# Gate and up from seven products of halves instead of eight, and one weight ring for the feed-forward

## The chip, the cores and the metric

The kernel runs on one core of one Trainium2 chip. The metric is the device time of one execution in microseconds, lower is better. Below, PE is the matrix engine TensorE, DVE is VectorE, ACT is ScalarE, POOL is GpSimd and SP is the engine whose queue starts the DMAs, in order.

## What is computed

One layer of a hybrid encoder over 2048 tokens of width 1024, in float32:

```
a    = rms_norm(h, ln_mix_pre)
proj = a @ w_in                      # split by columns into four mixers
mix  = concat([s5, hgrn2, fox, mlstm]) @ w_out
h    = h + rms_norm(mix, ln_mix_post)
a    = rms_norm(h, ln_ffn_pre)
ff   = (silu(a @ w_ffn_gate) * (a @ w_ffn_up)) @ w_ffn_down
h    = h + rms_norm(ff, ln_ffn_post)
```

w_ffn_gate and w_ffn_up are 1024 x 2816, w_ffn_down is 2816 x 1024, w_out 1024 x 1024. The change concerns the last four lines.

## The kernel before

**Stages.** The in-projection (`in_proj`, to about 840 us) runs over two halves of the tokens and, in each, over chunks of the columns of w_in; between chunks, hooks of a dictionary place other work (the S5 set-up, the mixers of the first tokens, and `first`, which does `Attn.pre(0)` and `Attn.proj(0)`). Then the feed-forward section runs over four blocks of 512 tokens: for block b the projection `attn.proj(b)`, the mixers of block b + 1, and the feed-forward `run(b)`, with `attn.pre(b + 1)` near its end. A scheduler of the language orders the instructions of each engine by its own timeline; the mixers of the next block are so spread between the products of this one. The last block has no mixers beside it.

**Precision.** Every float32 operand is kept as two parts, hi and lo, in the matmul type F32R, and a product takes three matmuls per 128 rows of depth: hi x hi, hi x lo, lo x hi. A weight tile is split at its first use (`split_load`): a copy by ACT gives hi (L89), a subtraction by POOL lo (L90); both parts are stored to DRAM, and later blocks load them (L85). Activations are split too (L104, L105) and both parts are transposed by PE, 4 tiles of 128 x 128 at a time (`transpose_parts`, L109), and copied out of PSUM by ACT and DVE (L112, L114).

**Attention projection** (`Attn.proj`, L1394): the first 512 columns of w_out for all four token tiles, then the second 512, one token tile after the other. After each tile follow its norm, the residual (its x loaded by L1427 into `b_xt`, a ring of two buffers), the store of h1 (L1429), the second norm (L1340, L1423, L1428, L69, L70, L1433) and the transposes.

**Feed-forward.** `gate_up` (L1477) makes for each of the 22 f tiles of 128 columns gate and up of all 512 tokens: 8 k x 3 parts x 2 = 48 matmuls of 512 columns. The first two f tiles of a block are done together in two halves of 256 columns, tokens 0 to 255 first (`cuts`). `down` (L1502) multiplies two f tiles at a time with w_ffn_down, 48 matmuls of 512 columns, and DVE adds the result to the accumulator (L1507). Gate and up weights go through a ring of 4 pairs of 128 x 1056, those of w_ffn_down through one of 4 pairs of 128 x 512.

## Time and profile before

| | us |
|---|---|
| median of 3 runs | 2833.97 |
| lowest and highest | 2827.44, 2839.25 |
| profiled execution, its time | 2835.35 |
| profiled execution, its span | 2833.6 |
| PE busy in the span | 2720.2 (96%) |
| DVE, POOL, ACT busy | 1598.5, 883.9, 830.7 |
| DMA moved | 605.11 MB, mean 214 GB/s |

The profile is one execution, taken by the hardware profiler. Busy times of the engines overlap. PEld is the loading of weights into PE, which runs beside its matmuls. Since the kernel has stages with different limits, tables by stage say more than the sums; a "window" is a stretch of the span in microseconds.

### The profile page before, as it was taken

The numbers are of one execution on the slowest core, as the hardware profiler recorded it, in microseconds if no ns is written. First come the engines' busy times: TensorE is split into PE (matmuls) and PEld (weight loads), VectorE is DVE, ScalarE is ACT, GpSimd is POOL, SyncE is SP. The second block draws the span as 40 slices with busy tenths as digits, with TensorE's granted clock in tenths as the row PEclk, the third lists the DMA queues.
The fourth block names the chain that finished last, engine by engine and source line by source line (L and its number), as shares of the span: only waits on it lengthen the run. The fifth ranks groups of instructions, "written<-read, shape, count | busy, mean of one in ns | idle before, by whom it ended". The sixth has DMA issues, their size and how long they took to land.

```text
span 2833.6 us, 40116 instructions
## 1 busy us (share of the span) xinstructions
PE 2720.2 (96%) x14678; PEld 2294.8 (81%) x14678; DVE 1598.5 (56%) x2587; ACT 830.7 (29%) x1596; POOL 883.9 (31%) x959
## 2 busy tenths in 40 slices
...
GB/s 201 207 255 135 179 289 171 169 176 154 254 191 313 279 270 252 242 295 230 288 164 210 192 207 212 153 264 210 214 184 188 196 170 230 273 211 193 190 192 139
DMA packets 323108, 605.11 MB, mean 214 GB/s; under 512 B 56160, under 2 KB 146144, under 8 KB 322656
## 3 DMA queue, kind: packets, MB, share of 16 engines
...
q0 software_dynamic: 1024, 0.07, 0.0%
...
## 4 chain that ended last, share of the span: by engine, by line
PE 72%; DVE 11%; DMA 9%; issue 3%; POOL 2%; SPq 2%; ACT 2%; DVEq 0%; POOLq 0%; ACTq 0%
PE pf L1477 30%; PE pf L1502 15%; PE pf L297 6%; PE pf L279 5%; PE pf L1394 3%; PE ps L912 2%; DMA g_h<-h_d 1%; DVE hQ L520 1%; DMA b_xt<-in_x_dram 1%; PE ps L896 1%; PE ps L895 1%; PE ps L837 1%; DVE hA L534 1%; PE pt L109 1%; DVE xl L105 1%
## 5 line engine op out<-in xcount | busy, mean ns | idle before, releaser
L1477 PE MATMUL pf<-b_ah,wl 128*128 128x512 f32 (+1 forms) x1536 | 580.0, 378 | 0.0
L1477 PE MATMUL pf<-b_ah,wh 128*128 128x512 f32 (+1 forms) x1536 | 579.6, 378 | 0.3 <-DMA wh<-wg2h 0.3
L1477 PE MATMUL pf<-b_al,wh 128*128 128x512 f32 (+1 forms) x1536 | 579.7, 379 | 0.0
L1502 PE MATMUL pf<-dh,g_h 128*128 128x512 f32 x1408 | 458.8, 395 | 1.9 <-DVE b_acc L1507 1.8
L1477 PEld LDWEIGHTS pf<-b_ah,wh 128*128 128x128 f32 x1536 | 290.4, 189 | 55.0 <-issue 0.4
L1477 PEld LDWEIGHTS pf<-b_ah,wl 128*128 128x128 f32 x1536 | 290.5, 189 | 54.8
L1477 PEld LDWEIGHTS pf<-b_al,wh 128*128 128x128 f32 x1536 | 289.6, 189 | 54.3
L1502 PEld LDWEIGHTS pf<-dh,g_h 128*128 128x128 f32 x1408 | 263.3, 188 | 57.5 <-DVE b_acc L1507 2.9
L1502 PE MATMUL pf<-dl,g_h 128*128 128x512 f32 x704 | 276.5, 393 | 0.0
L1507 DVE TENSOR_TENSOR b_acc<-b_acc,pf 128x512 f32<-128x512 f32 x320 | 215.6, 683 | 102.1 <-PE pf L1502 100.2
L909 POOL TENSOR_TENSOR f_accs<-f_accs,f_pe 128x512 f32<-128x512 f32 (+3 forms) x144 | 172.4, 1197 | 285.0 <-ACT f_pe L903 281.8
L90 POOL TENSOR_TENSOR wl<-wr,wh 128x1024 fp32r<-128x1024 f32 (+2 forms) x76 | 187.5, 2471 | 223.6 <-ACT wh L89 194.9
L905 DVE TENSOR_TENSOR f_pl<-f_pe,f_ph 128x512 fp32r<-128x512 f32 (+3 forms) x160 | 187.0, 1176 | 94.5 <-ACT f_ph L904 78.2
L297 PE MATMUL pf<-wh,aTh 128*128 128x256 f32 (+2 forms) x768 | 219.8, 287 | 2.6 <-ACT stg L323 1.6
L297 PE MATMUL pf<-wl,aTh 128*128 128x256 f32 (+2 forms) x768 | 221.4, 288 | 0.0
L297 PE MATMUL pf<-wh,aTl 128*128 128x256 f32 (+2 forms) x768 | 220.3, 287 | 0.0
L1482 DVE SCALAR_TENSOR_TENSOR g_th<-g_th,pf 128x512 f32<-128x512 f32 x88 | 60.3, 685 | 198.7 <-ACT g_th L1481 198.1
L1481 ACT ACTIVATE g_th<-pf 128x512 f32<-128x512 f32 x88 | 52.7, 599 | 399.1 <-PE pf L1477 399.0
L279 PE MATMUL pf<-aTh,wh 128*128 128x512 f32 (+1 forms) x400 | 159.8, 400 | 1.0 <-ACT hnz L304 1.0
L279 PE MATMUL pf<-aTl,wh 128*128 128x512 f32 (+1 forms) x400 | 158.3, 398 | 2.5 <-DVE aTl L114 2.5
L903 ACT ACTIVATE f_pe<-ps 128x512 f32<-128x512 f32 (+3 forms) x160 | 85.4, 534 | 252.7 <-PE ps L896 106.7
L279 PE MATMUL pf<-aTh,wl 128*128 128x512 f32 (+1 forms) x400 | 159.1, 398 | 0.0
...
## 6 DMA issues: line engine op xcount, KB each, us to landing
...
```

Of the source, the lines that this page charges most:

```text
L90: nc.gpsimd.tensor_tensor(lo, r, f32(hi), ALU.subtract)
L279: nc.tensor.matmul(l3(pt)[:, cut], lhsT=x[k][:, s], rhs=a[:, cut, k], start=(n == 0), stop=(n == 23))
L297: nc.tensor.matmul(pt[:, :w], lhsT=a[:, t, k], rhs=x[k], start=(n == 0), stop=(n == 23))
L903: nc.scalar.activation(pe[:, cs], pt[:, cs], AF.Exp)
L905: nc.vector.tensor_tensor(pl[:, cs], pe[:, cs], f32(ph[:, cs]), ALU.subtract)
L909: nc.gpsimd.tensor_tensor(accs[:, cs], accs[:, cs], pe[:, cs], ALU.add)
L912: nc.tensor.matmul(o, lhsT=w, rhs=r[:, cs], start=(kt + n == 0), stop=(kt + n == NK))
L1394: nc.tensor.matmul(pt, lhsT=a[:, t, k], rhs=w, start=(first and i == 0), stop=(last and i == 2))
L1477: nc.tensor.matmul(l3(pt)[:, s], lhsT=x[:, k], rhs=a[:, s, k], start=(k == 0 and i == 0), stop=(k == KD - 1 and i == 2))
L1482: nc.vector.scalar_tensor_tensor(th, th, 1.0, pts[0], ALU.add, ALU.mult)
L1502: nc.tensor.matmul(pt, lhsT=a[:, s], rhs=w[:, 0], start=(m == 0), stop=(m == 3 * len(fs) - 1))
L1507: nc.vector.tensor_tensor(acc[:, t, ns], acc[:, t, ns], pt, ALU.add)
```

## The change

It has seven parts.

1. Gate and up of two f tiles (a pair q) and both halves of the tokens are a 2 x 2 product of blocks: two halves of the depth (512), two f tiles. It is formed by the scheme of Strassen and Winograd from 7 products of sums instead of 8. A product is 4 k x 3 parts for gate and for up (m), with 256 columns; DVE puts them together with seven additions per pair, and ACT makes one copy.
2. The sums of weights are made in the in-projection (`FfnWeights.make`, 22 units, placed by hooks): two loads of 512 KB, four subtractions or additions of 128 x 512 on POOL, seven stores of 256 KB. Those of products 0, 2 and 5 are split at first use, and the parts stored; those of 1, 3, 4 and 6 are loaded and split in every block.
3. The sums of activations (`Attn.operands`) are made after every second token tile, three on DVE, one on POOL; 7 x 4 transposes follow. Both x tiles of the ring of two are held until then. No f tile is done in halves of the tokens any more.
4. Transposes are of plain float32, once; ACT copies hi out of PSUM, DVE subtracts lo.
5. One ring of 12 pairs of 128 x 512 takes all weights of the section, w_out too; the in-projection's ring is closed with it.
6. w_ffn_down and w_out are copied from DRAM to DRAM (30 copies of 512 KB) by the hooks of the in-projection, and read from the copies. `attn.proj(0)` moves out of the hook to the start of the section.
7. To make room, the mixers beside the feed-forward have fewer or smaller buffers (`hK` 3 and `hQ` 2 instead of 4, the fox pool `p` 4 instead of 5, the `f_KB` ring 2, and the like).

In PE's order at the start of the last block, the rows before are: L1394 is the projection, L109 the transposes, L1477 gate and up with 256 columns.

```order
L1394 MATMUL pf<-dl,b_ah 128x512
L109 MATMUL pt<-identr,xh 128x128 x4
L109 MATMUL pt<-identr,xl 128x128 x4
L109 MATMUL pt<-identr,xh 128x128 x4
L109 MATMUL pt<-identr,xl 128x128 x4
L1477 MATMUL pf<-b_ah,wh 128x256
L1477 MATMUL pf<-b_ah,wl 128x256
```

After, at the same place, L1436 is the projection, L111 the transposes and L1530 the products (g_h holds the sums, b_xt the plain tiles):

```order
L1436 MATMUL pf<-dl,b_U 128x512
L111 MATMUL pt<-ident,g_h 128x128 x4
L111 MATMUL pt<-ident,b_xt 128x128 x4
L111 MATMUL pt<-ident,g_h 128x128 x12
L111 MATMUL pt<-ident,b_xt 128x128 x8
L1530 MATMUL pf<-b_U,dh 128x256
L1530 MATMUL pf<-b_U,dl 128x256
```

Where 16 transposes stood behind the projection's last matmul, 28 stand now, and the first product behind them.

SP's order at the same start of the block, before (L1427 loads x, L1429 stores h1, L85 loads parts of weights):

```order
L1429 DMA h_d_228<-b_acc 128x1024 x2
L1427 DMA b_xt<-in_x_dram 128x1024
L85 DMA wh<-wg1h 128x1024
L85 DMA wl<-wg1l 128x1024
L85 DMA wh<-wu1h 128x1024
L85 DMA wl<-wu1l 128x1024
L1429 DMA h_d_228<-b_acc 128x1024
L85 DMA dh<-wd_0h 128x512
L85 DMA dl<-wd_0l 128x512
L85 DMA dh<-wd_0h 128x512
L85 DMA dl<-wd_0l 128x512
L1427 DMA b_xt<-in_x_dram 128x1024
```

After (L1469 loads x, L81 loads parts, L1376 loads a raw sum, L1618 loads h1 for the end):

```order
L81 DMA dh<-w_2_0h 128x512
L81 DMA dl<-w_2_0l 128x512
L81 DMA dh<-w_2_1h 128x512
L81 DMA dl<-w_2_1l 128x512
L1618 DMA g_h1s<-h_d_375 128x1024
L1376 DMA dl<-ws_3_0_66 128x512
L1376 DMA dl<-ws_3_1_67 128x512
L1376 DMA dl<-ws_4_0_68 128x512
L1376 DMA dl<-ws_4_1_69 128x512
L1376 DMA dl<-ws_6_0_72 128x512
L1376 DMA dl<-ws_6_1_73 128x512
L1469 DMA b_xt<-in_x_dram 128x1024 x2
```

The last two loads of x stood apart from each other, the second behind four loads of w_ffn_down; now both stand behind ten loads of weights of the next products.

SP's order in the third chunk of the in-projection, before (L88 loads w_in, L94 stores its parts; the last row is the third chunk's second load):

```order
L88 DMA wr<-in_w_in_dram 128x4x256
L1006 DMA s_cl<-in_s_lambda_re_dram 16x64 x2
L1010 DMA s_ldt<-in_s_log_dt_dram 128x16
L1067 DMA s_br<-in_s_b_re_dram 64x16x16
L94 DMA wi_1l<-wl 128x1024
L1067 DMA s_br<-in_s_b_re_dram 64x16x16
L1067 DMA s_bi<-in_s_b_im_dram 64x16x16 x2
L88 DMA wr<-in_w_in_dram 128x4x256
```

After (L1717 copies w_ffn_down; L100 loads w_in, L90 stores its parts):

```order
L1717 DMA wd_d<-in_w_ffn_down_dram 16x8192 x4
L90 DMA wi_0l<-wl 128x1024
L100 DMA wr<-in_w_in_dram 128x4x256
L1717 DMA wd_d<-in_w_ffn_down_dram 16x8192 x7
L1008 DMA s_cl<-in_s_lambda_re_dram 16x64 x2
```

Copies of w_ffn_down and w_out have come between the loads of w_in, 28 of the 30 of them ahead of the third chunk's second load.

The diff, cut to these parts:

```diff
...
-def split_load(c, pool, raw, tag, width, shape, src, key=None, part=None):
+def split_load(c, pool, tag, width, n, src, key=None, raw=None):
     nc = c.nc
-    n = shape[0] * shape[1]
     hi = pool.tile([P, width], F32R, name=tag + "h", tag=tag + "h")[:, 0:n]
     lo = pool.tile([P, width], F32R, name=tag + "l", tag=tag + "l")[:, 0:n]
     if key in c.parts:
-        a = part or 0
         for t, d in zip((hi, lo), c.parts[key]):
-            nc.sync.dma_start(f32(t), d[:, a:a + n])
-    else:
-        r = raw.tile([P, width], F32, name=tag + "r", tag=tag + "r")[:, 0:n]
-        nc.sync.dma_start(r.rearrange("p (k n) -> p k n", k=shape[0]), src)
-        nc.scalar.activation(hi, r, AF.Copy)
-        nc.gpsimd.tensor_tensor(lo, r, f32(hi), ALU.subtract)
-        if key is not None:
-            c.parts[key] = kept = [c.dram.tile([P, n], F32, name=f"{key}{x}") for x in "hl"]
-            for t, d in zip((hi, lo), kept):
-                nc.sync.dma_start(d, f32(t))
-    return [x.rearrange("p (k n) -> p k n", k=shape[0]) for x in (hi, lo)]
-def transpose_parts(c, pool, tag, x, dh, dl, eng):
+            nc.sync.dma_start(f32(t), d)
+        return hi, lo
+    x = f32(lo) if raw is None else raw.tile([P, WRING], F32, name="wr")[:, 0:n]
+    src(x)
+    nc.scalar.activation(hi, x, AF.Copy)
+    nc.gpsimd.tensor_tensor(lo, x, f32(hi), ALU.subtract)
+    if key is not None:
+        c.parts[key] = kept = [c.dram.tile([P, n], F32, name=f"{key}{x}") for x in "hl"]
+        for t, d in zip((hi, lo), kept):
+            nc.sync.dma_start(d, f32(t))
+    return hi, lo
...
-def transpose_parts(c, pool, tag, x, dh, dl, eng):
-    for h in range(0, KD, 4):
-        hs = slice(h * P, (h + 4) * P)
-        hi, lo = (c.phl.tile([P, 512], F32R, name=n, tag="hl") for n in ("xh", "xl"))
-        nc.scalar.activation(hi, x[:, hs], AF.Copy)
-        eng.tensor_tensor(lo, x[:, hs], f32(hi), ALU.subtract)
-        for src, dst in ((hi, dh), (lo, dl)):
-            pt = pool.tile([P, 512], F32R, name="pt", tag=tag)
-            for j in range(4):
-                nc.tensor.transpose(pt[:, j * P:(j + 1) * P], src[:, j * P:(j + 1) * P], c.identr)
-            pv = pt.rearrange("p (k t) -> p k t", k=4)
-            if src is hi:
-                nc.scalar.activation(dst[:, h:h + 4], pv, AF.Copy)
-            else:
-                nc.vector.tensor_copy(dst[:, h:h + 4], pv)
+    for h in range(0, x.shape[1] // P, 4):
+        pt = pool.tile([P, 512], F32, name="pt", tag=tag)
+        for j in range(4):
+            nc.tensor.transpose(pt[:, j * P:(j + 1) * P], x[:, (h + j) * P:(h + j + 1) * P], c.ident)
+        pv = pt.rearrange("p (k t) -> p k t", k=4)
+        nc.scalar.activation(dh[:, h:h + 4], pv, AF.Copy)
+        nc.vector.tensor_tensor(dl[:, h:h + 4], pv, f32(dh[:, h:h + 4]), ALU.subtract)
...
+class FfnWeights:
+    def __init__(self, c):
+        self.c = c
+        self.w = [x[0].rearrange("(k p) n -> p k n", p=P) for x in (c.w_ffn_gate, c.w_ffn_up)]
+        self.pairs = c.w_ffn_gate.shape[2] // (2 * P)
+        self.raw = {(q, i, m): c.dram.tile([P, 512], F32, name=f"ws{q}_{i}_{m}")
+                    for q in range(self.pairs) for i in range(7) for m in range(2)}
+    def make(self, pool, q, m):
+        nc = self.c.nc
+        r1, r2 = (pool.tile([P, D], F32, name=n, tag=n) for n in ("ws_1", "ws_2"))
+        for r, f in ((r1, 2 * q), (r2, 2 * q + 1)):
+            nc.sync.dma_start(r.rearrange("p (k n) -> p k n", k=KD), self.w[m][:, :, f * P:(f + 1) * P])
+        a, b = slice(0, 512), slice(512, D)
+        X11, X12, X21, X22 = r1[:, a], r1[:, b], r2[:, a], r2[:, b]
+        for i, s in ((0, X11), (2, X12), (5, X22)):
+            nc.sync.dma_start(self.raw[q, i, m], s)
+        for i, s, x, y, op in ((3, X11, X11, X21, ALU.subtract), (4, X21, X21, X22, ALU.add),
+                               (1, X22, X22, X11, ALU.subtract), (6, X12, X12, X22, ALU.subtract)):
+            nc.gpsimd.tensor_tensor(s, x, y, op)
+            nc.sync.dma_start(self.raw[q, i, m], s)
+    def load(self, q, i, m):
+        c = self.c
+        return split_load(c, c.pd, "d", 512, 512, lambda t: c.nc.sync.dma_start(t, self.raw[q, i, m]),
+                          f"w{q}_{i}_{m}" if i in (0, 2, 5) else None)
...
+        self.U = ctx.enter_context(c.tc.tile_pool(name="b_u", bufs=1, side="right", reuse_waits="tile")).tile(
+            [P, 14, D], F32R, name="b_U")
         self.row = None
-        self.pd = None
+    def pools(self, ctx):
+        self.p = ctx.enter_context(self.c.tc.tile_pool(name="b_a", bufs=1, side="right", reuse_waits="tile"))
+        self.ps = ctx.enter_context(self.c.tc.tile_pool(name="b_s", bufs=2, side="right", reuse_waits="tile"))
+    def y(self, t):
+        i = 2 * (2 * (t % 2)) + t // 2
+        return [self.U[:, j].rearrange("p (k t) -> p k t", k=KD) for j in (i, i + 2)]
+    def operand(self, i, j):
+        u = self.U[:, 2 * i + j].rearrange("p (d k t) -> p d k t", d=2, k=4)
+        return u[:, 0], u[:, 1]
...
-            for q in range(4):
-                if n == 1 and q >= 2 and self.pd is not None:
-                    for k in range(2 * q, 2 * q + 2):
-                        h, l = split_load(c, self.pd, self.pdr, "d", 512, (1, 512), wo[:, k:k + 1, ns],
-                                          f"wo{n}_{q}", k % 2 * 512)
-                        yield k, h[:, 0], l[:, 0]
-                else:
-                    h, l = split_load(c, c.pw, c.pwr, "w", WRING, (2, 512), wo[:, 2 * q:2 * q + 2, ns], f"wo{n}_{q}")
-                    for k in range(2):
-                        yield 2 * q + k, h[:, k], l[:, k]
+            for k in range(KD):
+                yield k, *split_load(c, c.pd, "d", 512, 512, from_dram(c, wo[:, k:k + 1, ns]), f"wo{n}_{k}")
...
-            transpose_parts(c, c.psS, "s", xt, ah[:, t], al[:, t], nc.vector)
+            xs.append(xt)
+            if t % 2:
+                self.operands(t // 2, *xs[-2:])
+    def operands(self, j, x, x1):
+        c, nc = self.c, self.c.nc
+        a, b = slice(0, 512), slice(512, D)
+        s1, s2 = self.row_tile(), self.row_tile()
+        T1, T2, T3, T4 = s1[:, a], s1[:, b], s2[:, a], s2[:, b]
+        nc.vector.tensor_tensor(T1, x1[:, a], x[:, a], ALU.subtract)
+        nc.vector.tensor_tensor(T2, x1[:, b], T1, ALU.subtract)
+        nc.gpsimd.tensor_tensor(T3, x1[:, b], x1[:, a], ALU.subtract)
+        nc.vector.tensor_tensor(T4, x[:, b], T2, ALU.subtract)
+        for i, v in enumerate((x[:, a], T2, x[:, b], T3, T1, T4, x1[:, b])):
+            transpose_parts(c, c.psS, "s", v, *self.operand(i, j))
...
-    attn.pd = pd = tp("g_wd", 4)
-    attn.pdr = tp("g_dr", 2)
+    c.pd = tp("g_w", 12)
     ph = tp("g_h", 4)
     p2 = tp("g_p2", 2)
+    p1 = tp("g_p1", 1)
...
-        def gate_up(fs, cuts):
-            job = []
-            for f in fs:
-                ws = [split_load(c, c.pw, c.pwr, "w", WRING, (KD, P), w[:, :, f * P:(f + 1) * P], f"w{n}{f}")
-                      for w, n in ((wg, "g"), (wu, "u"))]
-                job.append((f, ws, [ptile() for _ in ws]))
-            for s in cuts:
-                for f, ws, pts in job:
-                    for pt, (wh, wl) in zip(pts, ws):
-                        for k in range(KD):
-                            for i, (x, a) in enumerate(((wh, ah), (wl, ah), (wh, al))):
-                                nc.tensor.matmul(l3(pt)[:, s], lhsT=x[:, k], rhs=a[:, s, k],
...
+        def gate_up(q):
+            c1, c2 = (p1.tile([P, 2, 2, 256], F32, name=n) for n in ("g_c1", "g_c2"))
+            def product(i):
+                pt = ptile()
+                pv = pt.rearrange("p (m j t) -> p m j t", m=2, j=2)
+                for m in range(2):
+                    wh, wl = c.ffw.load(q, i, m)
+                    for k in range(4):
+                        for n, (w, d) in enumerate(((wh, 0), (wl, 0), (wh, 1))):
+                            nc.tensor.matmul(pv[:, m], lhsT=w[:, k * P:(k + 1) * P],
+                                             rhs=attn.U[:, 2 * i:2 * i + 2, d * 512 + k * P:d * 512 + (k + 1) * P],
+                                             start=(k == n == 0), stop=(k == 3 and n == 2))
+                return pt.rearrange("p (m t) -> p m t", m=2)
...
+            nc.scalar.activation(c1[:, 0], product(0), AF.Copy)
+            add(c1[:, 1], product(1), c1[:, 0])
+            add(c1[:, 0], product(2), c1[:, 0])
+            add(c2[:, 0], product(3), c1[:, 1])
+            pt = product(4)
+            add(c1[:, 1], pt, c1[:, 1])
+            add(c2[:, 1], pt, c2[:, 0])
+            add(c1[:, 1], product(6), c1[:, 1])
+            gated(2 * q, c1)
+            add(c2[:, 0], product(5), c2[:, 0])
+            gated(2 * q + 1, c2)
...
-        gate_up((0, 1), (slice(0, 2), slice(2, 4)))
-        for f in range(2, NF):
-            gate_up((f,), (slice(0, 4),))
-            if len(pend) == 3 and f < NF - 1:
-                down(pend[:2], pend[0][0] == 0)
+        for q in range(NF // 2):
+            gate_up(q)
+            if q:
+                down(pend[:2], q == 1)
                 pend = pend[2:]
...
+        c.pw = s.enter_context(tc.tile_pool(name="w_ring", bufs=4))
+        c.pwr = s.enter_context(tc.tile_pool(name="w_raw", bufs=2))
         setup, proj, row = in_proj(c, s)
+        stack = ExitStack()
+        pool = stack.enter_context(tc.tile_pool(name="w_sums", bufs=1, reuse_waits="tile"))
+        units = [(q, m) for q in range(c.ffw.pairs) for m in range(2)]
+        def sums(n):
+            def f():
+                for _ in range(min(n, len(units))):
+                    q, m = units.pop(0)
+                    c.ffw.make(pool, q, m)
+                    f = 2 * q + m
+                    nc.sync.dma_start(c.wd_d[f * P:(f + 1) * P], c.w_ffn_down[0, f * P:(f + 1) * P])
+                    if f < KD:
+                        nc.sync.dma_start(c.wo_d[f * P:(f + 1) * P], c.w_out[0, f * P:(f + 1) * P])
+            return f
+        def hooks(start, stop, n, d):
+            return {i: ([sums(n)] if start <= i < stop else []) + d.get(i, []) for i in range(11)}
...
+            sums(len(units))()
+            stack.close()
             attn = Attn(c, ctx)
-            rows = [row, lambda: attn.xtile("b_g0")]
-            attn.row = lambda: rows.pop()()
             attn.pre(0)
-            attn.proj(0)
...
-             {0: [lambda: lower_bound(c, const)], 2: [begin, hi(lambda c, b: s5_setup(c), 0)],
-              4: [hi(hgrn_mix, 0)], 8: [hi(mlstm_mix, 0)]})
+             hooks(3, 11, 1, {0: [lambda: lower_bound(c, const)], 2: [begin, hi(lambda c, b: s5_setup(c), 0)],
+                          4: [hi(hgrn_mix, 0)], 8: [hi(mlstm_mix, 0)]}))
         hi(s5_mix, 0)()
         hi(fox_mix, 0)()
         for h in range(1, c.NHALF):
-            proj(h, lambda: nullcontext(c.px), {4: [hi(hgrn_mix, 1)], 8: [first]})
+            proj(h, lambda: nullcontext(c.px), hooks(0, 7, 2, {4: [hi(hgrn_mix, 1)], 8: [first]}))
...
+        attn.pools(ctx)
         ffn = feed_forward(c, s, attn)
         c.side = "left"
         for b in range(NB):
-            if b:
-                attn.proj(b)
+            attn.proj(b)
...
```

## Rows read from the trace of the kernel before

**Rows 1.** The page: PE's busy time, share of the span, instructions.

```profile
PE 2720.2 (96%) x14678; PEld 2294.8 (81%) x14678; DVE 1598.5 (56%) x2587; ACT 830.7 (29%) x1596; POOL 883.9 (31%) x959
```

**Rows 2.** Windows: us; PE, PEld, DVE, ACT, POOL busy; PE clock; DMA share; GB/s.

```profile
840.00:1349.00 509.00, 489.46 (x2513) 406.15 (x2512) 336.39 (x484) 183.75 (x332) 277.71 (x217) 0.98 0.81 268
...
1933.00:2403.00 470.00, 468.45 (x2297) 381.62 (x2296) 271.05 (x405) 124.54 (x242) 118.68 (x119) 1.00 0.59 196
...
2451.00:2822.00 371.00, 369.54 (x1719) 304.70 (x1717) 116.85 (x171) 39.31 (x72) 8.76 (x10) 1.00 0.55 189
```

**Rows 3.** The chain of waits in the last block: start, us, what.

```profile
2489.33 10.90 PE pf L1502 x48
2500.23 22.30 PE pf L1477 x96
```

**Rows 4.** PE's timeline, 256-column matmuls: start, us, engine, line, operation.

```profile
848.81 0.28 PE L1477 MATMUL pf<-b_al,wh 128*128 128x256 f32 x1
...
851.64 0.28 PE L1477 MATMUL pf<-b_al,wh 128*128 128x256 f32 x1
...
2457.74 0.28 PE L1477 MATMUL pf<-b_al,wh 128*128 128x256 f32 x1
...
2461.44 0.28 PE L1477 MATMUL pf<-b_ah,wl 128*128 128x256 f32 x1
```

**Rows 5.** PE's groups by line and shape: busy, mean ns, idle before.

```profile
L109 PE MATMUL pt<-identr,xl 128*128 128x128 f32 x384 | 49.0, 250 | 17.6 <-DVE xl L105 14.3 <-ACT aTh L112 2.2 <-DVE aTl L114 0.9
```

**Rows 6.** PE's timeline at the start of the last block.

```profile
2450.05 0.46 PE L109 MATMUL pt<-identr,xh 128*128 128x128 f32 x4
...
2451.37 0.35 PE L1477 MATMUL pf<-b_ah,wh 128*128 128x256 f32 x1
```

**Rows 7.** PE's timeline, transposes of plain fp32 (the gates of mLSTM).

```profile
1423.06 0.60 PE L629 MATMUL ps<-ident,mlf 128*4 128x128 f32 x4
1423.50 0.60 PE L629 MATMUL ps<-ident,mg 128*4 128x128 f32 x4
```

**Rows 8.** The chain of waits at the start of the last block.

```profile
2443.00 3.69 DMA b_xt<-in_x_dram
...
2451.41 7.69 DMA b_xt<-in_x_dram
...
2459.23 1.29 DVE b_acc L1428
...
2462.70 1.30 DVE b_xt L1433
```

**Rows 9.** Windows in which DMA is full (columns as in Rows 2).

```profile
20.00:30.00 10.00, 9.03 (x68) 8.88 (x67) 8.02 (x11) 4.58 (x9) 9.18 (x11) 1.00 1.00 362
...
860.00:870.00 10.00, 10.00 (x58) 8.51 (x57) 1.38 (x2) 5.31 (x15) 9.92 (x10) 0.75 1.01 326
2451.00:2463.00 12.00, 11.81 (x107) 11.54 (x106) 6.64 (x10) 4.76 (x10) 2.58 (x4) 1.00 1.03 401
```

**Rows 10.** PE's timeline behind an idle stretch; in brackets the idle time.

```profile
1379.50 0.80 PE L1394 MATMUL pf<-wh,b_ah 128*128 128x512 f32 x1 [6.41 <-ACT junk L1340]
```

**Rows 11.** The window around it.

```profile
1378.00:1383.00 5.00, 3.50 (x8) 2.82 (x9) 2.46 (x4) 2.76 (x8) 0.25 (x1) 0.50 0.80 303
```

**Rows 12.** POOL's groups in block 0, by shape: busy, mean ns.

```profile
L90 POOL TENSOR_TENSOR wl<-wr,wh 128x1024 fp32r<-128x1024 f32 x42 | 101.0, 2405 | 98.1 <-ACT wh L89 83.9 <-PE ps L912 6.1 <-DMA wr<-in_w_ffn_up_dram 5.1
L90 POOL TENSOR_TENSOR dl<-dr,dh 128x512 fp32r<-128x512 f32 x44 | 61.7, 1411 | 66.8 <-ACT dh L89 43.9 <-DMA mk<-mk_d 20.3 <-DMA f_QA<-qa_d 2.5
```

**Rows 13.** SP's timeline: the third chunk's second load of w_in.

```profile
54.13 0.93 SPq L88 DMA_DIRECT2D wr<-in_w_in_dram  x1
```

**Rows 14.** The in-projection's matmuls: duration min/median/max, first and last start, shapes.

```profile
L297 PE MATMUL pf<-wh,aTh x768: 274/281/420, 91.5 to 839.3; 128*128 128x256 f32 x128, 128*128 128x264 f32 x32, 128*128 128x260 f32 x32
```

**Rows 15.** Windows of the in-projection (columns as in Rows 2).

```profile
0.00:92.00 92.00, 66.07 (x376) 56.44 (x377) 75.03 (x148) 57.15 (x90) 59.75 (x80) 0.93 0.63 205
...
690.00:840.00 150.00, 149.36 (x921) 131.55 (x921) 40.17 (x64) 48.25 (x92) 36.34 (x33) 1.00 0.69 223
```

114 lines of the change are left out of this document (60 added, 54 removed).

## The prediction, made before the changed kernel was run

> **What bounds the kernel now.** First the engine list of the page [rows 1]: TensorE (PE) is busy 2720.2 of 2833.6 us, so time leaves only if PE gets less work or waits less. Second the table by stage [rows 2], cut at the borders of the four token blocks: block 0's stage with its mixers (840 to 1349) has 509.00 us with PE busy 489.46, the like stage of block 2 has 470.00 with 468.45, the last block's 371.00 with 369.54. So PE idles 19.5 us where all weights are split for the first time, and 1.6 and 1.5 us later on: there, what PE is given is what it costs. Third the chain in the last block [rows 3]: per pair of f tiles 22.30 us for 96 gate/up matmuls and 10.90 us for 48 of the down product, back to back.
>
> All sums stand against the profiled execution, 2835.35 us (span 2833.6); it lies 1.4 us above the median 2833.97, which I take off at the end.
>
> **Gate and up: -127 us.** A pair now takes 7 products x 2 weights x 4 k x 3 parts = 168 matmuls of 256 columns instead of 96 of 512. What 256 columns cost stands in the trace, since before cuts the first two f tiles of a block in half: from 2457.74 to 2461.44 lie 32 steps, 0.1156 us each, and from 848.81 to 851.64 24 steps, 0.118 each [rows 4]. So 168 x 0.1156 = 19.4 us against 22.30, 2.9 less, times 44 pairs = -127; at 0.118 it is -109. The seven VectorE (DVE) sums and the copy that a pair gets have cover: a DVE operation on 128 x 1024 takes 1.29 us [rows 8], half of that for 512, so seven take 4.5 us of a pair's 30, and in the last block DVE is busy 116.85 of 371 us [rows 2].
> The Trainium skill, TensorE: Matmul & The Clock Gate, under The mechanism, says that a weight load overlaps running matmuls only where it goes to another row group; by its section on LDWEIGHTS a load of 128 columns is some 107 ns, and 44 x 72 more loads would then add an estimated 339 us. Rows 4 say otherwise: two steps of 256 columns (0.231) take no longer than the 22.30 / 96 = 0.232 us of one of 512, so nothing fixed is added to a matmul, and I leave this no chance.
>
> **Transposes: -11 us.** Before, hi and lo parts of 48 token tiles are transposed apart, 768 in all (two groups of 384, one of them in [rows 5]); in the last block 16 of them take 2450.05 to 2451.37, 0.083 each [rows 6]. After, 480 of plain fp32 (128 for x, 128 for y, 224 for operands); the row nearest to these is that of the gates, four in 0.44 us, 0.110 each [rows 7]. 768 x 0.083 - 480 x 0.110 = 64 - 53 = -11; bounds 0 and -20.
>
> **Block starts: +68 us.** Before, the start of the last block costs PE nothing: behind the last projection matmul the transposes start at 2450.05 and the first gate/up matmul at 2451.37 [rows 6]. But the chain of waits shows how late the fourth token tile is: its x is issued at 2451.41 and lands 7.69 us later, and from there 4.8 us (2459.23 to 2464.00, with 1.29 for the residual first and 1.30 for the norm last) pass until it is normed [rows 8]. PE fills this with the first halves, which need tiles 0 and 1 alone. After, no halves are left: every product takes its right side from all four tiles, from product 0 on. x tiles 2 and 3 need the two buffers that tiles 0 and 1 hold until operands(0) is transposed, and these transposes stand in PE's order behind the last projection matmul. In SP's order the two x loads (one row, x2) stand behind ten weight loads and one of h1, 3.1 MB, whose buffers the projection's second half frees at its end. With the x tiles that is 4.2 MB; at 362 to 401 GB/s [rows 9] it lands 10.4 to 11.6 us after the projection. Then comes the 4.8 us chain for tile 2 and again for tile 3, DVE taking one after the other: some 20 us until product 1 (T2 needs tile 3) can start. 28 transposes (3.1) and product 0 (24 x 0.1156 = 2.8) lie inside: about 14 us idle. After 6.41 us of idling PE's first matmul took 0.80 us, and the granted clock was 0.50, the lower level, 1.2 GHz, over the 5 us around it [rows 10, 11]; half of a stretch of 4 to 5 us is lost so, and I put 2 us on that, thus 16 us for blocks 1 to 3 (bounds 10 and 24), and 20 for block 0, where splits of these weights (1411 ns each on POOL [rows 12]) come in front. 3 x 16 + 20 = +68.
>
> **In-projection to feed-forward: +8 us.** The first projection of attention moves from a hook in the in-projection to the section's start, and its w_out tiles are loaded and split only there: 3.7 us for the first load to land, as the x at 2443.00 [rows 8], 1.4 for the split on POOL [rows 12], and some 3 for ACT's half of the split and a lower clock behind that. Bounds 0 and 15.
>
> **In-projection: +8 us.** 28 of the 30 DRAM-to-DRAM copies of w_ffn_down and w_out (0.52 MB each, 14.7 MB) and part of the first unit of weight sums stand in SP's order ahead of the second weight load of the third chunk, together some 16.4 MB. Before, that load is issued at 54.13 [rows 13] and the chunk's first matmul starts at 91.5 [rows 14]. Up to 92 us the DMA engines are busy 0.63, or 58 us [rows 15]. At the 326 GB/s of 860 to 870, where they are full [rows 9], the copies take 50 us: 108 us of DMA by 91.5, 16 late. PE idles 26 of these 92 us anyway [rows 15], and DVE and ACT lose half of the transposing; I take 8 off. Bounds -10 and +60. The 22 units of sums (4 POOL operations each, 1.4 us by [rows 12], 2.9 MB) spread over the hooks of both halves, where DMA is busy up to 0.69 [rows 15]; I price them at nothing, and if that cover is gone they belong to the rival below.
>
> **Splits in front of the mixers: +24 us.** Before, 86 splits (101.0 + 61.7 = 163 us of POOL) all fall in block 0 [rows 12], and PE idles 19.5 us there against 1.6 in block 2 [rows 2]: some 0.1 us per us of POOL splitting. After, block 0 has 154 weight tiles of gate and up, 44 of down and 16 of w_out to split, 214 x 1.41 = 302 us, 140 more: +14. The sums of products 1, 3, 4 and 6 are kept raw and split again in each block, 88 x 1.41 = 124 us. In blocks 1 and 2, which have mixers, I put 5 us on each: +10; in the last, where POOL is busy 8.76 us [rows 2], nothing. Bounds 0 and 38: that POOL's order puts splits behind f_accs work is what the upper end stands for.
>
> **The sum.** -127 - 11 + 68 + 8 + 8 + 24 = -30: 2835.35 - 30 - 1.4 = 2804 us.
>
> **The rivals.**
> A, the block starts are hidden: the scheduler's order is as I read it, but if the x tiles land early (weight buffers free one by one, not all at the end), the chain lies under the projection and the starts cost 2 to 3 us each: 68 becomes 10, 2746 us. For it: DMA has room, 0.59 and 0.55 in blocks 2 and 3 [rows 2]. Against it: the two x buffers.
> B, both costs at their upper ends: starts of 24 and 28 (+32) and three quarters of the way up on the splits (+10), 2846 us with nothing else moved; with the starts alone high, 2836. Both are no change.
> C, slower: a DRAM-to-DRAM copy passes each byte twice. At half of 326 GB/s the 16.4 MB take 100 us; the third chunk is due at 158 instead of 91.5, 66 late, less 8: +58 instead of +8, 2854 us. It exceeds the time of before from copies at 209 GB/s on (45 us late) and 2848 from 177. For it: the table of the page counts one set of 16 engines for reads and writes, and no row of before shows such a copy. Against it: 3.6 MB per 10 us go at 362 GB/s [rows 9], and a copy may count as one pass. Beside that stands the Trainium skill, DMA: Bandwidth & Descriptors, Specifications: some 358 GB/s of HBM per core; if both directions count, the copies take an estimated 92 us. Our 401 GB/s over 2451 to 2463 lie above that limit.
> D, the change doesn't do what it says (a 256-column step that doesn't halve): rows 4 exclude it.
>
> **Chances.** My forecast (one start of 10 to 20 us per block) 0.43, from 2765 to 2819; A 0.13; B 0.20; C 0.24. What a measurement can tell from no change is about 0.5%, 2820 to 2848: faster 0.43 + 0.13 = 0.56, same 0.20, slower 0.24. The range leaves out the lower half of A and the upper third of C: 2750 to 2868.
>
> **What the new profile would show.** Steps of 0.116 us in the products and 30.3 us per pair in the last block (the -127); from the last projection matmul of a block to product 1 some 20 us, the chain there led by the x loads, a lower granted clock right behind (A: under 7 us); the third chunk's first matmul near 100 us (C: past 140, with DMA at 1.00 until then); PE idle in block 0's stage some 14 us above 19.5, waiting for POOL splits. The forecast is wrong if products step at more than 0.12 us, if product 1 starts under 10 us after the projection, or if the in-projection ends past 870.

## The result, and the profile after

The changed kernel takes 2910.69 us (median of 4 runs, 2907.15 to 2914.6) against 2832.96 for the kernel before; the ratio is 1.0274 with a 95% interval of 1.0248 to 1.0300. I had forecast 2804 us, in a range of 2750 to 2868: the change makes the kernel slower, not faster, and the time lies outside the range.

The page of the changed kernel: the engines' busy times, and by engine the chain of work that ended last (`issue` is time for which the profile shows no wait, and a q marks an engine's queue):

```profile
PE 2650.7 (91%) x17174; PEld 2378.2 (82%) x17174; DVE 1898.4 (65%) x2879; ACT 1011.3 (35%) x1952; POOL 1470.7 (50%) x1399
...
PE 54%; DVE 17%; DMA 13%; POOL 7%; issue 5%; ACT 2%; SPq 2%; POOLq 0%; DVEq 0%; ACTq 0%
```

PE is busy 70 us less than in [rows 1] and yet the span is 79 us longer (2912.9): PE idles where it did not. Where, the windows tell (columns as in [rows 2]): the in-projection, then by turns the start of a block (from its first projection matmul to its first product) and the block itself.

```profile
0.00:827.00 827.00, 728.69 (x4626) 653.64 (x4626) 508.98 (x918) 267.18 (x519) 391.12 (x458) 0.94 0.84 277
827.00:897.00 70.00, 52.73 (x225) 43.56 (x226) 25.33 (x26) 29.12 (x59) 50.98 (x46) 0.87 0.85 307
897.00:1432.00 535.00, 476.39 (x3204) 432.09 (x3203) 394.41 (x557) 222.03 (x430) 362.85 (x304) 0.95 0.76 256
1432.00:1512.00 80.00, 53.16 (x243) 42.82 (x242) 38.60 (x50) 26.21 (x57) 28.26 (x34) 0.84 0.66 224
1512.00:1980.00 468.00, 450.68 (x3075) 406.30 (x3075) 351.15 (x530) 169.97 (x329) 237.45 (x213) 0.99 0.70 223
1980.00:2040.00 60.00, 49.15 (x226) 39.73 (x225) 29.46 (x33) 19.61 (x42) 22.60 (x28) 0.93 0.71 256
2040.00:2499.00 459.00, 448.33 (x2958) 402.27 (x2959) 334.58 (x484) 168.98 (x322) 231.33 (x190) 0.98 0.71 224
2499.00:2559.00 60.00, 48.45 (x224) 39.24 (x222) 29.03 (x31) 19.05 (x42) 23.13 (x28) 0.93 0.76 277
2559.00:2903.00 344.00, 343.12 (x2400) 318.55 (x2400) 180.71 (x246) 87.75 (x156) 119.57 (x93) 0.99 0.69 230
```

The kernel before, in order: the start of block 1, then those of blocks 2 and 3:

```profile
1349.00:1406.00 57.00, 50.59 (x240) 41.14 (x238) 26.27 (x31) 16.55 (x35) 13.50 (x23) 0.94 0.77 274
...
1885.00:1933.00 48.00, 47.63 (x228) 38.82 (x227) 24.30 (x29) 14.93 (x32) 9.12 (x18) 1.00 0.85 295
2403.00:2451.00 48.00, 47.79 (x232) 39.01 (x232) 25.87 (x30) 15.57 (x33) 9.38 (x19) 1.00 0.86 293
```

The last block, which has no mixers, is 27 us shorter (344 against 371). Blocks 1 and 2 are only 11 us shorter, and block 0 is 26 us longer (535 against 509), with 59 us of PE idle. Each start is longer: 80 against 57, 60 against 48 twice, 70 for the first against some 48. The in-projection is 35 us longer up to the first projection matmul (827 against 840 less the 48 us of the projection that stood in it). The products themselves save what their steps allow, as the chain in the last block shows:

```profile
2738.48 19.79 PE pf L1530 x168
2758.26 10.88 PE pf L1573 x48
```

168 matmuls take 19.79 us (0.1178 each) where 96 took 22.30 [rows 3].

### The profile page after: what moved, and what is told of

Its sections match the earlier page's. It is cut to its first block, busy times and chain, and to the rows that moved or that the text cites. A ratio compares the mean times of both kernels' runs of the same rounds, so it can differ in the third digit from the quotient of the medians.

```text
span 2912.9 us, 48560 instructions
## 1 busy us (share of the span) xinstructions
PE 2650.7 (91%) x17174; PEld 2378.2 (82%) x17174; DVE 1898.4 (65%) x2879; ACT 1011.3 (35%) x1952; POOL 1470.7 (50%) x1399
## 2 busy tenths in 40 slices
DMA packets 439570, 725.24 MB, mean 249 GB/s; under 512 B 69696, under 2 KB 159680, under 8 KB 438592
## 4 chain that ended last, share of the span: by engine, by line
PE 54%; DVE 17%; DMA 13%; POOL 7%; issue 5%; ACT 2%; SPq 2%; POOLq 0%; DVEq 0%; ACTq 0%
PE pf L1530 22%; PE pf L1573 11%; PE pf L1436 6%; DMA dl<-ws 4%; PE pf L279 3%; DVE hQ L520 2%; PE pf L297 2%; DMA ws<-ws 2%; POOL dl L86 1%; PE ps L914 1%; PE pt L111 1%; POOL ws L1370 1%; DVE f_pl L907 1%; DMA ws<-in_w_ffn_up_dram 1%; DVE hA L534 1%
## 5 line engine op out<-in xcount | busy, mean ns | idle before, releaser
L86 POOL TENSOR_TENSOR dl<-dl,dh 128x512 fp32r<-128x512 f32 x478 | 671.7, 1422 | 556.7 <-ACT dh L85 511.0
L1530 PE MATMUL pf<-b_U,dh 128*128 128x256 f32 x4928 | 922.5, 284 | 6.4 <-DVE b_acc L1578 3.6
L1530 PEld LDWEIGHTS pf<-b_U,dh 128*128 128x128 f32 x4928 | 782.2, 192 | 19.7 <-ACT b_U L113 4.5
L1530 PE MATMUL pf<-b_U,dl 128*128 128x256 f32 x2464 | 700.2, 284 | 0.0
L1530 PEld LDWEIGHTS pf<-b_U,dl 128*128 128x128 f32 x2464 | 472.9, 192 | 5.0
L85 ACT ACTIVATE dh<-dl 128x512 fp32r<-128x512 f32 x478 | 294.0, 628 | 506.8 <-DMA dl<-ws 367.9
L1536 DVE TENSOR_TENSOR g_c<-pf,g_c 128x512 f32<-128x512 f32 x308 | 207.4, 685 | 213.9 <-PE pf L1530 212.5
L1573 PEld LDWEIGHTS pf<-dh,g_h 128*128 128x128 f32 x1408 | 268.8, 191 | 91.5 <-DVE b_acc L1576 15.6
L907 DVE TENSOR_TENSOR f_pl<-f_pe,f_ph 128x512 fp32r<-128x512 f32 (+3 forms) x160 | 181.3, 1140 | 72.1 <-ACT f_ph L906 71.4
L1436 PE MATMUL pf<-dh,b_U 128*128 128x512 f32 x512 | 160.9, 399 | 23.4 <-ACT junk L1343 15.5
L297 PEld LDWEIGHTS pf<-wh,aTh 128*128 128x128 f32 x768 | 151.8, 198 | 12.4 <-ACT stg L323 7.9
L1370 POOL TENSOR_TENSOR ws<-ws,ws 128x512 f32<-128x512 f32 x66 | 91.2, 1381 | 133.5 <-DMA ws<-ws 103.9
```

What stands on the lines that cost most here:

```text
L85: nc.scalar.activation(hi, x, AF.Copy)
L86: nc.gpsimd.tensor_tensor(lo, x, f32(hi), ALU.subtract)
L297: nc.tensor.matmul(pt[:, :w], lhsT=a[:, t, k], rhs=x[k], start=(n == 0), stop=(n == 23))
L907: nc.vector.tensor_tensor(pl[:, cs], pe[:, cs], f32(ph[:, cs]), ALU.subtract)
L1370: nc.gpsimd.tensor_tensor(s, x, y, op)
L1436: nc.tensor.matmul(pt, lhsT=a[:, k], rhs=w, start=(first and i == 0), stop=(last and i == 2))
```

## Experiments

**Are the repeated splits the cost, or the smaller mixers?** Theory S: the sums of products 1, 3, 4 and 6 are split in every block, 88 times, on ACT and POOL. Theory M: the mixers lose by the buffers taken from them. e1 takes the splits away:

```diff
 def load(self, q, i, m):
+    if i in (1, 3, 4, 6):
+        hi = c.pd.tile([P, 512], F32R, name="dh", tag="dh")
+        c.nc.sync.dma_start(f32(hi), self.raw[q, i, m])
+        return hi, hi
```

> The changed kernel, but the weight sums of products 1, 3, 4 and 6 are not split: their raw tile is loaded once and stands for hi and lo both (the low parts of these weights are left out). The loads stay as they are; 88 copies on ACT and 88 subtractions on POOL per block go (some 55 and 125 us of busy time each). Theory S (these splits stand in front of the mixers' work and slow it): PE idle falls from 52 to about 25 us in block 0's stage, from 17 to 6 in block 1's and from 11 to 3 in block 2's, the block starts lose 1 to 3 us each; in all 2910 becomes 2840 to 2860. Theory M (the mixers lose time because their buffers were cut to make room): the idle times stay, 2900 to 2912.

Measured: 2805.5 us, 0.9906 of before (0.9886 to 0.9926): 105 us less than the changed kernel. S holds, and by more than it said: PE idles 13 us in block 0's stage, not 25. e2 puts the changed `hgrn_mix`, `mlstm_mix`, `fox_mix` and `s5_mix`, with their smaller buffers, into the kernel before, and nothing else:

```diff
-        nk = 4
+        nk, nq = (4, 4) if c.side == "right" else (3, 2)
...
-                                  (("const", 1), ("q", 2), ("kv", 2), ("p", 5), ("p2", 2)))
+                                  (("const", 1), ("q", 2), ("kv", 2), ("p", 5 if c.side == "right" else 4), ("p2", 2)))
```

> The kernel before, with nothing of the change but the smaller mixers (fewer hK, hQ, fox p and f_KB buffers, one buffer for the S5 loads, gate tiles of mLSTM in halves). Theory M: 40 to 60 us slower than before, 2875 to 2895, with PE waits on DVE and DMA in the stages of the blocks. Theory S: within 10 us of before, 2825 to 2845.

Measured: 2843.3 us, 1.0039 (1.0025 to 1.0053), 11 us more. M is real but a tenth of the matter. In e2's trace the loss lies at the starts of blocks 1 and 2, 61.5 and 54.7 us instead of 57.3 and 48.0.

**ACT or POOL?** e6 leaves the copies on ACT and takes only POOL's subtraction away:

```diff
     nc.scalar.activation(hi, x, AF.Copy)
+    if key is None:
+        return hi, hi
     nc.gpsimd.tensor_tensor(lo, x, f32(hi), ALU.subtract)
```

> The changed kernel, but of the splits of products 1, 3, 4 and 6 (and of every other split whose parts are not kept) only the copy on ACT is left; the subtraction on POOL is left out and hi stands for lo (the low parts are left out). Theory P (POOL's queue, and POOL beside DVE, is what costs): 2800 to 2820, as e1, block 0's stage at 470 to 480 us. Rival A (the copies on ACT, or waiting for the raw tile to land before it can be split, cost it): 2870 to 2910, block 0's stage over 510.

Measured: 2800.8 us, 0.9866 (0.9829 to 0.9904), no slower than e1. So the copies cost nothing that these runs show, and it hangs on POOL's subtractions. Windows of e6, blocks 0 to 3:

```profile
884.50:1349.00 464.50, 454.49 (x3204) 417.45 (x3205) 355.45 (x563) 229.66 (x438) 251.16 (x226) 0.99 0.84 290
1425.00:1874.00 449.00, 444.44 (x3077) 404.77 (x3078) 325.34 (x531) 172.69 (x329) 120.56 (x133) 1.00 0.72 228
1933.00:2374.00 441.00, 438.88 (x2958) 397.65 (x2959) 315.04 (x484) 170.52 (x321) 114.76 (x110) 0.99 0.73 229
2434.00:2776.00 342.00, 341.60 (x2400) 320.20 (x2399) 164.86 (x246) 91.09 (x155) 9.84 (x14) 0.99 0.70 227
```

Block 0 loses 70 us, blocks 1 and 2 19 and 18, the last, where nothing stands beside the products, about 1. These are 108 of the 127 us between the two profiled executions; the rest lies before block 0 and at the other starts, and the medians are 110 us apart. In block 0, 49 of the 70 are idle time of PE and 22 are PE's own: the same 3204 matmuls are busy 476 us at a granted clock of 0.95 and 454 at 0.99. And DVE, with the same work (557 and 563 operations), is busy 394 us with the splits and 355 without. Every edit of a split also lets the scheduler order the block anew: PE's and DVE's order in block 0 differ between the changed kernel, e6, e8 and e12. How much of a stage's difference is order, no run shows; but e1 and e6, two further orders, agree within 3 us in each of the four stages.

**How does POOL reach PE?** PE waits in block 0 hardly ever for POOL (2.6 of its 59 us of idle time); 47 us end with DVE. The longest of these waits (us, times, longest) in the changed kernel, then in e6 and, from further below, in e12:

```profile
PE ps L914 <- DVE f_pl L907: 12.8, 4, 6.7
```

```profile
PE ps L916 <- DVE f_pl L909: 0.6, 1, 0.6
```

```profile
PE ps L916 <- DVE f_pl L909: 9.9, 4, 3.6
```

The timelines of DVE and POOL in the changed kernel:

```profile
1027.10 10.42 DVE L907 TENSOR_TENSOR f_pl<-f_pe,f_ph 128x512 fp32r<-128x512 f32 x1
...
1038.04 0.68 DVE L907 TENSOR_TENSOR f_pl<-f_pe,f_ph 128x512 fp32r<-128x512 f32 x1
```

```profile
1027.08 1.27 POOL L911 TENSOR_TENSOR f_accs<-f_accs,f_pe 128x512 f32<-128x512 f32 x1
1028.32 4.98 POOL L86 TENSOR_TENSOR dl<-dl,dh 128x512 fp32r<-128x512 f32 x4
1033.27 1.25 POOL L911 TENSOR_TENSOR f_accs<-f_accs,f_pe 128x512 f32<-128x512 f32 x1
1034.49 2.47 POOL L86 TENSOR_TENSOR dl<-dl,dh 128x512 fp32r<-128x512 f32 x2
```

A subtraction of FoX that takes 0.68 us a little later takes 10.42 here, beside eight POOL operations in a row, and ends 0.6 us after the last of them (1036.96). DVE's groups in block 0 (busy, mean ns), first of the changed kernel, then of e6:

```profile
L1578 DVE TENSOR_TENSOR b_acc<-b_acc,pf 128x512 f32<-128x512 f32 x80 | 52.8, 678 | 9.5 <-PE pf L1573 9.4
...
L907 DVE TENSOR_TENSOR f_pl<-f_pe,f_ph 128x512 fp32r<-128x512 f32 x20 | 34.1, 1707 | 12.6 <-ACT f_ph L906 12.6
L1543 DVE TENSOR_TENSOR g_th<-g_th,g_c 128x512 f32<-128x512 f32 x22 | 25.4, 1155 | 0.2
```

```profile
L1580 DVE TENSOR_TENSOR b_acc<-b_acc,pf 128x512 f32<-128x512 f32 x77 | 51.3, 680 | 4.5 <-PE pf L1575 4.3
L909 DVE TENSOR_TENSOR f_pl<-f_pe,f_ph 128x512 fp32r<-128x512 f32 x20 | 23.2, 1166 | 7.2 <-ACT f_ph L908 7.2
L1545 DVE TENSOR_TENSOR g_th<-g_th,g_c 128x512 f32<-128x512 f32 x22 | 18.2, 829 | 0.2
```

The add that reads one side from PSUM (pf) takes 680 ns either way; these two, which read two tiles of SBUF, take 1.4 and 1.5 times as long in the changed kernel (of the others L520 takes 985 ns instead of 638, L516 829 and 818). What lengthens them is POOL at the same moment: in the traces of the kernel before, the changed one, e6, e8 and e12, 212 operations of these two groups (L907 and L1543 of the changed kernel, 128x512) ran with POOL idle, and took 664 to 723 ns; of the 700 beside a working POOL 524 took more than 700 ns, up to 10417. The Trainium skill, GPSIMD Engine Reference, Specifications, has the rule: GpSimd shares its SBUF interfaces with VectorE, and they contend where a DVE instruction has two SBUF inputs. The trace agrees, and the price here is 39 us more of DVE for 112 us more of POOL. The change also made new work of that kind: the gating that read pf before now reads g_c.

e12 tells the occupation of POOL from the waiting of products for their low parts: POOL subtracts as often, and no matmul reads the result (the low parts are left out).

```diff
     nc.gpsimd.tensor_tensor(lo, x, f32(hi), ALU.subtract)
+    if key is None:
+        return hi, hi
```

> The changed kernel, where POOL still makes the low parts of the sums of products 1, 3, 4 and 6, with the same 88 subtractions per block, but no matmul reads them: hi stands for lo in the products (the low parts are left out of the result). It tells what e6 could not: whether the 110 us hang on POOL and the units beside it being busy, or on products waiting for their low part. Theory O (occupation: POOL's queue, and DVE operations that take longer beside POOL): 2890 to 2912, block 0's stage at 520 to 535 us. Rival L (the path from landing over ACT and POOL to the matmul): 2800 to 2830, block 0's stage under 485 us.

Measured: 2880.2 us (2874 to 2894), 1.0169 (1.0120 to 1.0219), 10 us under what theory O asked and far above rival L. So most of it stays with POOL merely busy: 79 of the 110 us by the medians, 107 of 127 by the profiled executions, and 56 of 71 in block 0, whose 520 us are within O's range. The other 20 to 31 us go with the products' wait for low parts. The FoX subtraction is as long as ever in e12's block 0:

```profile
L909 DVE TENSOR_TENSOR f_pl<-f_pe,f_ph 128x512 fp32r<-128x512 f32 x20 | 38.2, 1913 | 9.7 <-ACT f_ph L908 9.7
```

O has two halves, and the idle times tell them apart in part. The mixers' own work on POOL, late in its queue, shows little: in block 0 DVE idles 9.3 us behind POOL in e12 and 9.5 in e6, ACT 22.8 and 15.9, PE not at all. DVE's busy time is 47 us longer (402 against 355). e8 moves the same 88 subtractions to DVE:

```diff
-    nc.gpsimd.tensor_tensor(lo, x, f32(hi), ALU.subtract)
+    (nc.vector if key is None else nc.gpsimd).tensor_tensor(lo, x, f32(hi), ALU.subtract)
```

> The changed kernel with the subtractions of the splits of products 1, 3, 4 and 6 on DVE instead of POOL (88 per block, 0.69 us each, some 61 us of DVE work more per block). Theory P: POOL has room and DVE operations are no longer stretched, but DVE has more to do: block 0's stage falls from 535 to 490 to 515 us, in all 2850 to 2890. Rival A: nothing is won on POOL and DVE gets 61 us more per block: 2920 to 2970.

Measured: 2887.8 us, 1.0174 (1.0133 to 1.0215): 23 us less than the changed kernel, within theory P's range for the time. Block 0 of e8, then of e12 (profiled execution 2894.4 us):

```profile
893.00:1422.00 529.00, 480.34 (x3204) 434.97 (x3203) 419.40 (x637) 221.60 (x429) 253.81 (x224) 0.94 0.77 259
```

```profile
898.00:1418.00 520.00, 471.73 (x3202) 427.26 (x3203) 402.07 (x557) 225.41 (x429) 362.59 (x304) 0.96 0.77 259
```

POOL is 109 us freer in e8, and the stage is 6 us shorter, not the 20 to 45 that theory P asked; the gain is spread over all stages, at most 6 us in one. Against e6 DVE is busy 64 us longer when it does the subtractions and 39 when POOL does them: in this stage, where PE's waits end with DVE (40 of 50 us in e8), little is won by moving them.

**Splitting once.** e5 keeps the parts of all products:

```diff
-                          f"w{q}_{i}_{m}" if i in (0, 2, 5) else None)
+                          f"w{q}_{i}_{m}")
```

> The changed kernel, but the parts of all seven products are kept: products 1, 3, 4 and 6 too are split once, in block 0, and their parts stored (46 MB more) and loaded in blocks 1 to 3 (23 MB more each). Theory S (the repeated splits cost what e1 gave back): the stages of blocks 1 and 2 lose the 18 and 16 us that they lost in e1 (468.6 to 451, 458.3 to 443), the last 1; block 0's stage stays at 535 us, as it splits as before; in all 2873 to 2880. Rival D (the additional DMA takes it back): blocks 1 and 2 stay within 5 us of 468 and 458, or block 0 grows by over 15 us; 2895 or more.

Measured: 2887.9 us, 1.0180 (1.0150 to 1.0209). Blocks 1 and 2 fall to 452 and 448 us, nearly as far as S said for the first and two thirds of it for the second; but block 0, which has 46 MB more to store, grows from 535 to 541 at a DMA share of 0.93 instead of 0.76, and the start behind it by 4. The time lies between the two forecasts, and 7 of the 27 us between the profiled executions are in the in-projection, which e5 does not change.

**The starts of the blocks.** In the last block PE waits so (its timeline):

```profile
2557.53 1.09 PE L111 MATMUL pt<-ident,b_xt 128*128 128x128 f32 x4 [11.07 <-DVE b_xt L1475]
2559.30 0.58 PE L1530 MATMUL pf<-b_U,dh 128*128 128x256 f32 x1 [0.69 <-ACT b_U L113]
```

e7 gives x tiles 2 and 3 two buffers of their own:

```diff
+        self.px2 = ctx.enter_context(self.c.tc.tile_pool(name="b_x2", bufs=2, side="right", reuse_waits="tile"))
-            xt = self.xtile("b_xt")
+            xt = self.xtile("b_xt") if t < 2 else self.px2.tile([P, D], F32, name="b_xu", tag="xu")
-    c.pd = tp("g_w", 12)
+    c.pd = tp("g_w", 10)
```

> The changed kernel with two more buffers for the x tiles of the attention projection, used for token tiles 2 and 3, paid for by two of the twelve weight pairs; these loads no longer wait for the transposes of tiles 0 and 1. Theory X (the starts of the blocks wait for x): PE idle from the projection to the products falls from 11 to 12 us to under 5 in blocks 2 and 3, and from 27 to under 20 in block 1; in all 15 to 30 us, 2880 to 2895. Rival Y (the splits of the first products in POOL's queue in front of the norms): the idle times stay at 9 or more; 2900 to 2915.

Measured: 2886.5 us, 1.0178 (1.0147 to 1.0208). Starts of blocks 1 to 3 of e7:

```profile
1422.00:1497.00 75.00, 53.20 (x243) 42.62 (x241) 39.33 (x50) 25.70 (x56) 25.84 (x31) 0.86 0.71 237
1958.00:2014.00 56.00, 50.96 (x226) 42.16 (x225) 30.22 (x33) 18.47 (x40) 18.59 (x24) 0.94 0.76 271
2474.00:2529.00 55.00, 49.13 (x229) 39.81 (x227) 29.43 (x31) 18.00 (x39) 18.79 (x23) 1.00 0.85 305
```

Idle falls from 27 to 22, from 11 to 5 and from 12 to 6 us. The time is as X said, but X holds for half of the idle time in blocks 2 and 3 and a fifth in block 1, and its bounds (under 5, under 20) are just missed. The three starts make 15 of the 28 us between the profiled executions; 11 and 8 lie in the stages of blocks 0 and 1, which X says nothing of. In block 1 most of the rest is another wait, for loads of h1 that end block 0 and stand behind the loads of w_out (chain of waits of the changed kernel):

```profile
1457.23 5.51 DMA dh<-wo_7h
...
1462.76 5.95 DMA g_h<-h_d
```

In the changed kernel it kept PE idle for 15.5 us, 6.4 in the kernel before [rows 10].

e10 is e5 and e7 together.

> The changed kernel with the parts of all products kept (as in e5) and the two more x buffers with ten weight pairs (as in e7). If the two causes are apart from each other, their gains add up: 2911 - 23 - 24 = 2864, within 8 us. If the smaller ring or the additional DMA makes them collide: 2875 or more.

Measured: 2880.7 us, 1.0156 (1.0133 to 1.0178): 17 more than the sum of the two gains allows. Blocks 1 to 3 keep them; block 0 pays:

```profile
893.00:1448.00 555.00, 494.61 (x3220) 440.60 (x3221) 391.26 (x575) 228.25 (x445) 366.14 (x312) 0.93 0.93 323
```

20 us more than without either. PE idles as long as there (60 us), 19 of it now before products whose weight is not yet split (11.9 behind ACT's copy, 6.9 behind POOL's subtraction), and its matmuls take 18 us more, at a clock of 0.93 instead of 0.95. Which of the two, ten pairs instead of twelve or DMA at 0.93, does it, the runs don't tell.

**The in-projection.** e3 leaves the DRAM-to-DRAM copies out (w_out and w_ffn_down are read from `c.ffw.raw` tiles instead):

```diff
-                    nc.sync.dma_start(c.wd_d[f * P:(f + 1) * P], c.w_ffn_down[0, f * P:(f + 1) * P])
-                    if f < KD:
-                        nc.sync.dma_start(c.wo_d[f * P:(f + 1) * P], c.w_out[0, f * P:(f + 1) * P])
```

> The changed kernel without the 30 DRAM-to-DRAM copies; w_out and w_ffn_down are read from stored weight sums instead (same sizes, other numbers). Theory C (the copies crowd the in-projection): the first matmul of the first attention projection comes 10 to 20 us earlier than 827, the whole at 2890 to 2900. Theory W (the weight sums do it): it moves by less than 5 us, 2905 to 2912.

Measured: 2906.1 us, 1.0266 (1.0229 to 1.0304); the first projection matmul comes at 825.3 instead of 827.1. That is no difference: in the eight traces whose in-projection is that of the changed kernel (it, e1, e5 to e8, e10 and e12) this matmul comes between 818.4 and 827.2, with PE's order the same. So the copies cost nothing by then that shows. e4 leaves the weight sums out (`make` does nothing), e11 only their POOL operations:

```diff
-            nc.gpsimd.tensor_tensor(s, x, y, op)
             nc.sync.dma_start(self.raw[q, i, m], s)
```

> The changed kernel without the making of weight sums (22 units of two loads, four POOL operations and seven stores are left out; the products read rows of the copied w_ffn_down instead, same sizes, other numbers); the copies stay. Theory W: the first matmul of the first attention projection comes 15 to 25 us earlier than 827, the whole at 2885 to 2895. Theory C: less than 5 us, 2905 to 2912.

> The changed kernel without the 88 additions and subtractions on POOL in the making of weight sums (the unsummed halves are stored in their place, so the numbers differ); loads and stores of the 22 units stay. Theory P (POOL work, beside which DVE operations take longer): as e4, the first matmul of the first attention projection at 800 to 810 instead of 827, in all 2875 to 2890. Rival T (the 63 MB of loads and stores): 820 to 830, 2900 to 2912.

Measured: e4 2877.1 us, 1.0155 (1.0124 to 1.0185), the first projection matmul at 804.0; e11 2896.7 us, 1.0226 (1.0201 to 1.0250), at 812.9. Against the spread of 818.4 to 827.2 the sums hold up the in-projection by 14 to 23 us, 5 to 14 of them by POOL's 88 operations; the 9 us between e11 and e4 go with 63 MB of DMA. So both theories of e11 had a part. The other 11 us of e4's gain fall in the blocks, whose loads it also changed; they are not divided further.

**One part alone.** e9 is the kernel before with the new `transpose_parts` and nothing else:

```diff
-        eng.tensor_tensor(lo, x[:, hs], f32(hi), ALU.subtract)
...
-                nc.tensor.transpose(pt[:, j * P:(j + 1) * P], src[:, j * P:(j + 1) * P], c.identr)
+            nc.tensor.transpose(pt[:, j * P:(j + 1) * P], x[:, (h + j) * P:(h + j + 1) * P], c.ident)
```

> The kernel before with the new transposes alone: plain float32 is transposed once (384 instead of 768 of 128x128), ACT copies hi out of PSUM and DVE subtracts lo; the splits in front of the transposes (64 on DVE, 32 on POOL, 96 on ACT) go. Term of the prediction: 768 x 0.083 - 384 x 0.110 = 22 us less PE work, so 2805 to 2825. Rival: PE waited at these places for other reasons, and the time stays within 8 us of before, 2826 to 2842.

Measured, in 6 runs: 2808.3 us (2806.41 to 2814.3), 0.9907 (0.9889 to 0.9924). It leaves nothing out, and is faster than both kernels; PE is busy 22.2 us less (2698.0). The in-projection up to its projection, first of e9, then of before: 11.5 us shorter, 9 of them PE's work.

```profile
0.00:683.00 683.00, 619.70 (x4034) 558.57 (x4034) 450.82 (x883) 250.19 (x484) 271.12 (x371) 0.96 0.58 194
```

```profile
0.00:695.00 695.00, 628.37 (x4164) 566.18 (x4165) 468.22 (x917) 266.09 (x518) 276.50 (x374) 0.96 0.58 192
```

## Why the prediction was wrong, step by step

- **Gate and up, -127.** Right in kind, mis-sized: 19.79 us per 168 instead of 19.4 makes 44 x 2.51 = -110, what the step of 0.118 in [rows 4] gave. I chose the quicker of two rows without a reason.
- **Transposes, -11.** For 384 instead of 768 the same working gives 22 us, and e9 measures 22.2 less of PE and some 26 of time. The working holds; the changed kernel has 96 more of them, and its own saving was not measured apart.
- **Block starts, +68, and the transition, +8.** Measured against before: 22 + 22 + 12 + 12 = 68 us, and 8 us of waiting from the last in-projection matmul (819.1) to the first of the projection (827.1). From the projection's last matmul (2542.8) to the start of product 0 are 16.5 us, 11 of them one wait. Product 1 starts 23 to 24 us after the projection in blocks 1 to 3, where I had said some 20. The mechanism, x behind the weights, is half of the waiting in blocks 2 and 3 and a fifth in block 1 (e7). The sum is right by luck: in blocks 1 to 3 I had 16 each, and in block 1 the wait for h1, which I had not seen, fills what the others lack.
- **In-projection, +8.** Its last matmul comes 27 us late in the changed kernel's trace (819.1 against 839.7 - 48.0), 19 to 27 in the eight traces named under e3. For the copies I had the right place: plain transposes alone bring the third chunk's first matmul from 91.5 [rows 14] to 80.2 (e9), in the changed kernel it is back at 91.7, and without the copies (e3) at 86.3. So there they cost some 5 us, where I had 8, and nothing of it shows at the end. What was wrong is the sums, which I priced at nothing because DMA had room; they cost 14 to 23, part of it by POOL's operations. Rival C, copies at half rate, falls: the first 92 us moved 329 GB/s at a DMA share of 0.96, 343 GB/s of busy time, and e3 moves 15.7 MB less, each copy counted once (709.51 against 725.24 MB). The time came out slower, but not by it. The third chunk of the changed kernel, then of e9 and of e3:

```profile
L297 PE MATMUL pf<-wh,aTh x768: 276/282/582, 91.7 to 818.9; 128*128 128x256 f32 x128, 128*128 128x264 f32 x32, 128*128 128x260 f32 x32
```

```profile
L290 PE MATMUL pf<-wh,aTh x768: 276/282/564, 80.2 to 824.3; 128*128 128x256 f32 x128, 128*128 128x264 f32 x32, 128*128 128x260 f32 x32
```

```profile
L297 PE MATMUL pf<-wh,aTh x768: 275/282/582, 86.3 to 817.2; 128*128 128x256 f32 x128, 128*128 128x264 f32 x32, 128*128 128x260 f32 x32
```

- **Splits in front of the mixers, +24, bounds 0 and 38: the step that failed.** e6 takes 110 us off: 70, 19, 18 and 1 by blocks. I took 0.1 us per us of POOL from block 0's idle time in [rows 2], as if it were proportional, and 5 us each for blocks 1 and 2. I had expected PE to idle some 14 us above 19.5 in block 0, waiting for POOL's splits; it idles 59, 47 of them waiting for DVE. POOL's work does not only stand in POOL's queue, it stretches DVE's (39 us in block 0), and DVE was busy 336 of 509 us already; with the sums of the products it came to 394 of 535. The trace of before had it, in rows that I did not read: the same DVE group in block 0, beside the splits, and in block 2, without.

```profile
L1487 DVE SCALAR_TENSOR_TENSOR g_h<-g_th,g_h 128x512 fp32r<-128x512 f32 x22 | 38.3, 1741 | 13.5 <-ACT g_h L1486 13.3
```

```profile
L1487 DVE SCALAR_TENSOR_TENSOR g_h<-g_th,g_h 128x512 fp32r<-128x512 f32 x22 | 15.8, 717 | 5.1 <-ACT g_h L1486 4.9
```

- **The smaller mixers.** They had no term at all; e2 puts 11 us on them.

Put together: -110 for the products, +76 for starts and transition, +27 for the in-projection and +110 for the splits make +103, where 78 were measured. The transposes and the smaller mixers are not added again: the in-projection and the starts are measured with both in them (e9's 11.5 us, e2's starts). Of the 25 us too many 17 are in block 0: e6's is 44.5 us shorter than that of the kernel before (464.5 against 509.0), where the products save 27.6 (110 / 4), so what e6 takes away the kernel before paid in part too. The other 8 are not divided further. In the in-projection, e4 without sums still ends 4.5 us later than the kernel before (796.2 against 791.7), though plain transposes save some 11 there: these 16 us, and the rest of the waits at the starts (5 to 6 us each, under e7), stay open.

None of my three signs of being wrong came about (steps of 0.1178 us, product 1 at 23 us, the in-projection's end at 819): none of them looked at DVE or POOL.

Rivals A and D did not come about; B named the right cost, the splits, at a third of its size (24 + 10 against 110).
